# Ten instead of eight groups of a second feed-forward with weight sums made ahead: a decoder layer on one core of Trainium2

## The chip, the cores and the metric

The kernel runs on one core of a Trainium2 chip. The metric is the device time in microseconds (us) of one execution, and the median of several executions is compared. One execution was also taken by the hardware profiler. Its span is the time from the first to the last instruction of the program.

The engines are named as in the profile: PE is the matrix engine (PEld its weight loads), DVE the vector engine, ACT the scalar engine, POOL the general one, and SP the engine whose queue issues nearly all transfers.

## What is computed

The reference is one decoder layer in float32 on 256 tokens of width 2048.

```python
h = layer_norm(alpha * h + 0.5 * swiglu(h, w_ffn1_gu, w_ffn1_down))      # first feed-forward
rq, rk, rv, rg, aq, ak, av, gate_r, gate_a = split(h @ w_in)
ret = (silu(rg) * head_group_norm(retention(rotary(rq), rotary(rk), rv))) @ w_ret_out
att = windowed_attention(rotary(aq), rotary(ak), av, sinks) @ w_att_out
mixed = (sigmoid(gate_r) * ret + sigmoid(gate_a) * att) @ w_mix_out
h = layer_norm(alpha * h + mixed)
h = layer_norm(alpha * h + 0.5 * swiglu(h, w_ffn2_gu, w_ffn2_down))      # second feed-forward
h = layer_norm(alpha * h + sigmoid(h @ w_ple_gate) * (p @ w_ple_proj))
```

There are 8 retention heads, 16 attention heads, and 5632 columns in each feed-forward.

## The kernel before

**Products in float32.** Every float32 operand is split (`split`, L97): ACT casts it to a high part (L98) and DVE subtracts that to get the low part (L99). One product then takes three matmuls (`Sum.add`, L374 to L376). In the profile `hw_in_f` and `lw_in_f` are the high and low parts of a chunk of the input weights; `hf_gu`, `lf_gu` are those of the feed-forward's weights.

**Kinds of weight units.** All weights are listed in `plan` in the order of their use. A pair of blocks of a feed-forward's up projection comes as one of three kinds. A plain pair (P) is two units of `Single`, of 12 matmuls each. `Seven` (S) multiplies the two-by-two blocks with seven products instead of eight, which is 21 matmuls instead of 24. It needs four sums of weight blocks, which DVE forms, ACT casts and DVE splits (L160 to L186). `Prepared` (D) does the same 21 matmuls, but loads the four sums, already split, from DRAM (L198 to L206).

**Sums made ahead.** `sums_ahead` (L219) makes the sums of one or more groups; one group is one D pair of one block. It is a generator that advances by one piece at a time.

```python
        pairs = [[Chunk(k) for k in items[0]]]                 # L226: two loads of 512 KB
        for _ in range(wait):
            yield
        ...
            dve.tensor_tensor(t1, b11, b12, ALU.add)           # L238
            dve.tensor_tensor(t3, b12, b22, ALU.add)           # L239
            act.copy(uh, u)                                    # L240: a cast on ACT
            yield from pause()                                 # `every` times
            dve.tensor_tensor(t2, b11, t3, ALU.add)            # L242
            dve.tensor_tensor(t4, t2, b21, ALU.add)            # L243
            act.copy(vh, v)                                    # L244: a cast on ACT
            ...                                                # L246: loads of the next group
            yield from pause()
            dve.tensor_tensor(ul, u, uh, ALU.subtract)         # L248
```

After another pause DVE makes `vl` (L250) and SP is given two stores of 512 KB (L252). After a last pause come two more (L255), and the next group's L238 follows in the same piece.

**Steps.** The order on every engine is that of the program text. After each weight unit the kernel calls `done`, which issues loads and splits (one cast on ACT and one subtraction on DVE) for units some way ahead, and then `run_side` (L310). `run_side` issues one job of the list `side` and then one piece of the first generator in `lazy`. One such call is called a step here. The generators are queued at L1124 to L1127, and steps are counted from there:

| steps | weight units |
|---|---|
| 1 to 32 | `rqk`: retention's queries and keys |
| 33 to 56 | `rv`: retention's values |
| 57 to 88 | `rg`: retention's gates, eight units for each of four pairs of heads |
| 89 to 92 | `av`: attention's values |
| 93 to 112 | `aqk`: attention's queries and keys, five groups of four |

Before the change the generators take steps 1 to 20 (two groups, `wait` 3, `every` 2), 21 to 31 (a rotary table), 32 to 58 (three groups, 2 and 2) and 59 to 78 (one group, 3 and 4). Two more groups are made during the mixing projection (L1444).

**Side jobs in the gates.** For each pair of heads (h, h+1), nine jobs stand in `side` (L1229 to L1251):

| job | what | steps, by pair of heads |
|---|---|---|
| 1 | scores of h (PE `rs`, DVE `rsc`) | 57, 69, 78, 87 |
| 2 | split of the scores of h (`rsp`), scores of h+1 | 58, 70, 79, 88 |
| 3 | split of the scores of h+1, values of h (PE `ro`, DVE `gst`) | 59, 71, 80, 89 |
| 4 | normalisation of h (DVE, `ron` L1193), values of h+1 | 60, 72, 81, 90 |
| 5 | normalisation of h+1 | 61, 73, 82, 91 |
| 6 | `ron` of h times its gate (DVE L1203) | 65, 74, 83, 92 |
| 7 | transposes of h (PE `rt` L1212), `ron` of h+1 times its gate | 66, 75, 84, 93 |
| 8 | ACT and DVE take h out (`rett`, L1223 and L1224), transposes of h+1 | 67, 76, 85, 94 |
| 9 | the same for h+1 | 68, 77, 86, 95 |

The gate of a pair (`rgs`, L1243) is two ACT instructions, issued after the last of the pair's eight units, and so after the steps 64, 72, 80 and 88.

**Slots.** All these tiles live in 46 slots. `slots_for_weights` tells how many of them the planner (`fill`, L260) may fill with weights. A D pair takes 6 slots to load and 7 while it is used; an S pair takes 2 and 7. In the second feed-forward a block j that has D pairs sets this to 32 minus j (L940), and it stays until the next setting.

**The second feed-forward** has eleven blocks j of its up projection, of 8 pairs each (L839). Even blocks run as PPSSPSSP. Odd ones run as PPSPSPSP, or as PPSDSDSP if they are in `AHEAD_BLOCKS`. Eight transposes (`f2t`, L893) follow two units into the next block.

Of the kernel before, what the change touches and what calls it, by code (L numbers as in the profile page):

```python
# [39 lines left out]


AHEAD = (4, 5)
AHEAD_BLOCKS = (1, 3, 5, 7)
AHEAD_SLOTS = 32

SEVEN_DOWN = (6, 7, 8, 9)
# [9 lines left out]
def layer(ctx: ExitStack, tc: tile.TileContext, io):  # L56
# [16 lines left out]
    def slot(shape, dt, name):  # L73
        return slots.tile(shape, dt, tag="slot", name=name)
# [144 lines left out]
    def sums_ahead(items, wait, every):  # L219


        def pause():
            for _ in range(every):
                yield

        pairs = [[Chunk(k) for k in items[0]]]  # L226
        for _ in range(wait):
            yield
        for j, (key, _) in enumerate(items):
            a, b = pairs.pop()  # L230
            b11, b21, b12, b22 = a.of(a.raw, 0), a.of(a.raw, 1), b.of(b.raw, 0), b.of(b.raw, 1)
            u, v = (slot([P, 2, 512], F32, w + a.name) for w in "uv")
            t1, t3, t2, t4 = (x.rearrange("p (g n) -> p g n", g=2) for x in (u[:, 0], u[:, 1], v[:, 0], v[:, 1]))
            parts = [slot([P, 2, 512], F32R, w + a.name) for w in ("hu", "lu", "hv", "lv")]
            uh, ul, vh, vl = parts
            away = [dram.tile([P, 2, 512], F32, name=f"{w}{a.name}") for w in ("hud", "lud", "hvd", "lvd")]
            put_by_sums[key] = away
            dve.tensor_tensor(t1, b11, b12, ALU.add)  # L238
            dve.tensor_tensor(t3, b12, b22, ALU.add)  # L239
            act.copy(uh, u)  # L240
# [3 lines that stand above are left out]
            act.copy(vh, v)  # L244
            if j + 1 < len(items):
                pairs.append([Chunk(k) for k in items[j + 1]])  # L246
# [3 lines that stand above are left out]
            dve.tensor_tensor(vl, v, vh, ALU.subtract)  # L250
            for e in range(2):
                sync.dma_start(away[e], parts[e].bitcast(F32))  # L252
            yield from pause()
            for e in range(2, 4):
                sync.dma_start(away[e], parts[e].bitcast(F32))  # L255
# [44 lines left out]
    def slots_for_weights(n, ahead=45, far=90):  # L300
        room.update(slots=n, ahead=ahead, far=far)
# [5 lines left out]
    lazy = []  # L307
# [152 lines left out]
    def forms_of(parts, name):  # L460
        hi, lo = (slot([P, 8, P], F32R, name + w) for w in "hl")
        return seven_forms(whole(parts, name + "w"), hi, lo)

    def units_of(order, sevens, ahead=()):

        sevens, ahead = list(sevens), list(ahead)
        plain = [p for p in range(KD // 2) if p not in sevens + ahead]
        of = {"S": sevens, "D": ahead, "P": plain}
        return [(kind, of[kind].pop(0)) for kind in order]
# [369 lines left out]
    def gu_units(name, j):  # L839
        if j == 0:  # L840
            return [("P", p) for p in range(KD // 2)]
        if name == "f2" and j in AHEAD_BLOCKS:
            return units_of("PPSDSDSP", SEVEN[:3], AHEAD)
# [3 lines left out]
    def gu_keys(name, j):  # L847
        return lambda n, p: (name + "_gu", j, n, p)
# [26 lines left out]
    def ffn(name, i, ht, norm, keep, residual, keepers, away):  # L875
# [28 lines left out]
        for j in range(KF // 4):  # L904
# [19 lines left out]
            def before(u, j=j, offset=KD // 2 - len(units)):  # L924
# [7 lines left out]
                if j == 0 and u == 7:  # L932
# [3 lines left out]
                    if name == "f2":  # L936
                        g = AHEAD[0] // 2
                        made[g] = forms_of([ht[:, 4 * g : 4 * g + 4, :]], f"{name}f{g}")
                if name == "f2" and j in AHEAD_BLOCKS and u == 0:
                    slots_for_weights(AHEAD_SLOTS - j)  # L940
# [151 lines left out]
    def mixers(ht, norm, residual, keepers, away):  # L1092
# [29 lines left out]
        slots_for_weights(14)  # L1122
        ahead = [(gu_keys("f2", j)(0, p), gu_keys("f2", j)(1, p)) for j in AHEAD_BLOCKS for p in AHEAD]
        lazy.append(sums_ahead(ahead[:2], 3, 2))  # L1124
        lazy.append(rotary_table("a"))
        lazy.append(sums_ahead(ahead[2:5], 2, 2))
        lazy.append(sums_ahead(ahead[5:6], 3, 4))  # L1127
        for grp in range(8):
            ps = banks(f"rqk{grp}")
            features_out([(("w_in_f", grp), ps)], KD, both_halves)  # L1130
# [310 lines left out]

        lhs = lambda k: of_pairs(mix_t, k)
        slots_for_weights(16)
        lazy.append(sums_ahead(ahead[6:], 3, 2))  # L1444
        for blk in range(3):
            if blk == 2:
                load_for_norm(1)
# [195 lines left out]
    with tc.manual_schedule():  # L1643
        dve.memset(warm, 0.0)
        for eps, v in roots.items():
            dve.memset(v, 4.0 * eps)
        act.activation(warm, warm, AF.Silu)
        plan_ffn("f1")
        plan.extend(Single(("w_pp", blk, 0)) for blk in range(2))
        plan_mixers()  # L1650
        plan.extend(Single(("w_pp", blk, 0)) for blk in range(2, 4))
        plan_ffn("f2")
        for blk in range(4):
            plan_tokens(("w_pg", blk), KD)
        kept = sorted({p // 2 for p in SEVEN})
        warm_up()
        norm = ffn("f1", 0, ht, None, x_parts, x_columns, (), rows[0])
        norm = mixers(norm.new, norm, rows[0], kept, rows[1])
        norm = ffn("f2", 2, norm.new, norm, norm.keep, rows[1], (), None)
        embedding(norm.new, norm, norm.y)  # L1660
        assert not (plan or loaded or ready or side or lazy) and not room["used"]
# [100 lines left out]
```

## Time and profile before

| | before |
|---|---|
| median of 3 runs | 2276.8 us (2276.71 to 2277.43) |
| profiled execution, its own time | 2277.11 us |
| its span | 2275.3 us |
| granted PE clock, mean | 0.999 |

The profile's page gives the busy time of each engine and its share of the span. Matmuls are pipelined, so the duration of one (some 0.39 us) is longer than the distance from one to the next. The view of waits lists for each instruction group which engine it waited for: us in total, times, longest us. The timeline lists instructions in order of time: start us, duration us, engine, line, operation, tile written and tiles read, and in square brackets the engine's idle time before it with what ended it. The chain of waits lists pieces of the path that ended last: start us, us, what.

### The profile page before, as it was taken

What the parts mean: (1) busy time and instruction counts of PE and PEld (TensorE: products, weight loads), DVE (VectorE), ACT (ScalarE), POOL (GpSimd) and SP (SyncE); (2) the same over time, 40 slices, a digit from 0 to 9 for tenths busy, and PEclk for the clock granted to TensorE, in tenths of its full rate; (3) what the DMA queues carried; (4) which work ended last, traced back from release to release, by engine and by line L of the source; (5) the groups of instructions that cost most, each with busy time, mean ns of one, the idle gap of its engine ahead of it and who ended that gap; (6) DMA issues with size and microseconds to landing.
All of it is one profiled execution on the core that took longest, in us unless ns stands there. A gap on an engine that the chain in (4) does not pass through costs nothing.

```text
span 2275.3 us, 29066 instructions
## 1 busy us (share of the span) xinstructions
PE 2263.4 (99%) x10495; PEld 1880.2 (83%) x10495; DVE 1980.6 (87%) x2561; ACT 1219.5 (54%) x1485; POOL 2.2 (0%) x9
## 2 busy tenths in 40 slices
PE   9999999999999999999999999999999999999998
PEld 8888888888888888888778888888888888888876
DVE  7999999999888887787789787789999999889877
ACT  6555555556554444544566454555565556555543
POOL 0000000000000000000000000000000000000000
PEclk9999999999999999999999999999999999999999
DMA  8666665665576789655456568787767766555772
GB/s 300 204 203 198 197 210 179 205 204 189 208 287 247 269 306 306 221 169 165 139 157 224 183 212 273 287 287 237 262 218 250 259 197 216 192 214 190 287 263 75
DMA packets 207592, 505.75 MB, mean 222 GB/s; under 512 B 16076, under 2 KB 19788, under 8 KB 207448
## 3 DMA queue, kind: packets, MB, share of 16 engines
q1 hardware_dynamic: 205320, 501.06, 65.6%
q10 hardware_dynamic: 2128, 2.84, 0.4%
q8 instruction: 82, 1.34, 0.2%
q14 instruction: 62, 0.51, 0.1%
HBM read 478.67 MB, written 25.17 MB: 221 GB/s over the span
## 4 chain that ended last, share of the span: by engine, by line
PE 97%; DVE 1%; DMA 1%; issue 0%; ACT 0%; POOL 0%; ACTq 0%; DVEq 0%; POOLq 0%
PE f1g L375 3%; PE f1g L374 3%; PE f1g L376 3%; PE f2g L376 3%; PE f2g L374 3%; PE f2g L375 3%; PE rqk L325 3%; PE f1u L374 2%; PE f1u L376 2%; PE f1u L375 2%; PE f2u L374 2%; PE f2u L376 2%; PE f2u L375 2%; PE aqk L325 2%; PE f1d L374 2%; PE f1d L376 2%
## 5 line engine op out<-in xcount | busy, mean ns | idle before, releaser
L99 DVE TENSOR_TENSOR lf_gu<-rf_gu,hf_gu 128x1024 fp32r<-128x1024 f32 (+1 forms) x276 | 325.3, 1210 | 13.3 <-ACT hf_gu L98 12.2
L98 ACT CAST hf_gu<-rf_gu 128x1024 fp32r<-128x1024 f32 (+1 forms) x276 | 275.4, 1042 | 30.1 <-DMA rf_gu<-in_f_gu 26.2
L99 DVE TENSOR_TENSOR lf_down<-rf_down,hf_down 128x1024 fp32r<-128x1024 f32 x152 | 181.2, 1219 | 22.6 <-ACT hf_down L98 19.6
L99 DVE TENSOR_TENSOR lw_in_f<-rw_in_f,hw_in_f 128x1024 fp32r<-128x1024 f32 x140 | 167.2, 1218 | 34.5 <-ACT hw_in_f L98 34.5
L98 ACT CAST hf_down<-rf_down 128x1024 fp32r<-128x1024 f32 x152 | 155.4, 1050 | 76.7 <-DMA rf_down<-in_f_down 22.4
L98 ACT CAST huf_gu<-uf_gu 128x1024 fp32r<-128x1024 f32 x70 | 73.7, 1053 | 145.3 <-DVE uf_gu L171 138.8
L98 ACT CAST hw_in_f<-rw_in_f 128x1024 fp32r<-128x1024 f32 x140 | 139.8, 1049 | 2.9 <-DMA rw_in_f<-in_w_in_f 2.3
L374 PE MATMUL f1g<-hf_gu,xt 128*128 128x512 f32 x247 | 96.5, 391 | 0.0
L375 PE MATMUL f1g<-hf_gu,xt 128*128 128x512 f32 x247 | 96.3, 390 | 0.0
L376 PE MATMUL f1g<-lf_gu,xt 128*128 128x512 f32 x247 | 96.3, 390 | 0.0
L98 ACT CAST hvf_gu<-vf_gu 128x1024 fp32r<-128x1024 f32 x70 | 73.8, 1054 | 29.2 <-DVE vf_gu L173 27.8
L950 ACT ACTIVATE eve<-eve 128x1024 f32<-128x1024 f32 x20 | 21.2, 1062 | 126.5 <-DVE eve L949 126.5
L374 PE MATMUL f2g<-hf_gu,ht 128*128 128x512 f32 x223 | 86.9, 390 | 0.0
L376 PE MATMUL f2g<-lf_gu,ht 128*128 128x512 f32 x223 | 86.9, 390 | 0.0
L375 PE MATMUL f2g<-hf_gu,ht 128*128 128x512 f32 x223 | 86.8, 389 | 0.0
L99 DVE TENSOR_TENSOR luf_gu<-uf_gu,huf_gu 128x1024 fp32r<-128x1024 f32 x70 | 85.2, 1218 | 0.0
L99 DVE TENSOR_TENSOR lvf_gu<-vf_gu,hvf_gu 128x1024 fp32r<-128x1024 f32 x70 | 85.2, 1218 | 0.0
L374 PE MATMUL f1u<-hf_gu,xt 128*128 128x512 f32 x212 | 83.5, 394 | 0.0
L376 PE MATMUL f1u<-lf_gu,xt 128*128 128x512 f32 x212 | 82.6, 390 | 0.0
L375 PE MATMUL f1u<-hf_gu,xt 128*128 128x512 f32 x212 | 82.5, 389 | 0.0
L374 PE MATMUL f2u<-hf_gu,ht 128*128 128x512 f32 x180 | 71.3, 396 | 0.0
L376 PE MATMUL f2u<-lf_gu,ht 128*128 128x512 f32 x180 | 70.1, 389 | 0.0
(1439 smaller groups left out, 6511.6 us busy)
## 6 DMA issues: line engine op xcount, KB each, us to landing
rf_gu<-in_f_gu SPq DMA_DIRECT2D x358, 512.0 KB
rf_down<-in_f_down SPq DMA_DIRECT2D x176, 512.0 KB
rw_in_f<-in_w_in_f SPq DMA_DIRECT2D x148, 512.0 KB
rw_rv<-in_w_rv SPq DMA_DIRECT2D x32, 512.0 KB
rw_ret<-in_w_ret SPq DMA_DIRECT2D x32, 512.0 KB
rw_mix<-in_w_mix SPq DMA_DIRECT2D x32, 512.0 KB
rw_pg<-in_w_pg SPq DMA_DIRECT2D x32, 512.0 KB
rw_att<-in_w_att SPq DMA_DIRECT2D x16, 512.0 KB
```

The lines of the kernel that those rows point to most:

```text
L98: act.copy(dst_hi, src)
L99: (lo_engine or dve).tensor_tensor(dst_lo, src, dst_hi, ALU.subtract)
L325: pe.matmul(ps[f], hi[:, kk, f * P : (f + 1) * P], rhs(k), start=k == 0, stop=k == n_k - 1,)
L374: pe.matmul(o, al, bh, start=first, stop=False)
L375: pe.matmul(o, ah, bh, start=False, stop=False)
L376: pe.matmul(o, ah, bl, start=False, stop=self.left == 0)
L950: act.activation(g, g, AF.Silu)
```

## The change

The second feed-forward's block 9 gets two D pairs in place of two plain pairs, so that five blocks with two groups each take prepared sums. The ten groups are made in a new division. The first five stay where they were. The sixth, seventh and eighth are made by one generator that is queued where the sixth was, with `wait` 2 and `every` 3 in place of 3 and 4. The last two are made during the mixing projection, with the same numbers as the last two before.

```diff
 AHEAD = (4, 5)
-AHEAD_BLOCKS = (1, 3, 5, 7)
+AHEAD_BLOCKS = (1, 3, 5, 7, 9)
...
         lazy.append(sums_ahead(ahead[:2], 3, 2))
         lazy.append(rotary_table("a"))
         lazy.append(sums_ahead(ahead[2:5], 2, 2))
-        lazy.append(sums_ahead(ahead[5:6], 3, 4))
+        lazy.append(sums_ahead(ahead[5:8], 2, 3))
...
         slots_for_weights(16)
-        lazy.append(sums_ahead(ahead[6:], 3, 2))
+        lazy.append(sums_ahead(ahead[8:], 3, 2))
```

## The prediction

> **What bounds the kernel now.** I read the page first, then the waits of PE, then the chain.
>
> ```profile
> span 2275.3 us, 29066 instructions
> PE 2263.4 (99%) x10495; PEld 1880.2 (83%) x10495; DVE 1980.6 (87%) x2561; ACT 1219.5 (54%) x1485; POOL 2.2 (0%) x9
> ```
>
> ```profile
> PE plnt L1529 <- DVE plnm L1524: 2.9, 1, 2.9
> ...
> PE rt L1212 <- DVE ron L1203: 0.2, 1, 0.2
> ```
>
> PE is busy for 2263.4 of 2275.3 us, and its longest wait is 2.9 us at the very end. So a matmul taken out is worth its full time, and a new wait of PE costs its full length, since no slack of PE exists later to take it back. Of the few waits one lies where the change adds work: the transposes `rt` of the retention heads wait for DVE's `ron`. DVE is the second engine at 87%.
>
> **What block 9 saves.** In the chain the transposes `f2t` mark the blocks of the second feed-forward. From one mark to the next is one block, from the third unit of one to the second of the next.
>
> ```profile
> 1780.58 0.88 PE f2t L893 x8
> ...
> 1821.59 0.88 PE f2t L893 x8
> ...
> 1863.29 0.88 PE f2t L893 x8
> ...
> 1905.66 0.88 PE f2t L893 x8
> ```
>
> Block 7 with two D pairs takes 1821.59 - 1780.58 = 41.01 us; block 9 without takes 1905.66 - 1863.29 = 42.37. The change makes block 9 like block 7: two pairs of 21 matmuls in place of two of 24, six fewer in all, **-1.36 us**. The left-hand sums that D pairs need exist already.
>
> Does a D pair cost block 9 a wait? Its two pairs load 2.75 MB each (512 + 256 + 4 x 512 KB) in place of 1 MB. In block 7 that shows on DVE, ahead of the S pair that follows the second D pair:
>
> ```profile
> 1795.89 0.69 DVE L170 TENSOR_TENSOR uf_gu<-rf_gu,rf_gu 128x512 f32<-128x512 f32 x1 [4.01 <-DMA rf_gu<-in_f_gu]
> ...
> 1801.50 1.22 DVE L99 TENSOR_TENSOR lvf_gu<-vf_gu,hvf_gu 128x1024 fp32r<-128x1024 f32 x1
> ```
>
> DVE stood idle for 4.01 us and was done with that S pair at 1802.72. At 1.36 / 6 = 0.227 us a matmul, four units of 12 and this one of 21 lie between its beginning and the mark at 1821.59, so PE begins it at 1805.9: 3.2 us in hand, and PE waits for none. Block 9 has 32 - 9 = 23 slots where block 7 has 25, so some of its loads start a unit later. I take 0 for this; the ends are 0 and +1.6 (one unit of 21 matmuls, 4.76 us, less the 3.2 in hand). The two groups during the mixing projection are as many as before: 0.
>
> **What the gates have to take.** The new generator again starts at step 59. With `wait` 2 and `every` 3 a group takes 12 steps: first sums (L238, L239 and a cast) at 61, 73, 85; second sums (L242, L243 and a cast) at 64, 76, 88; `ul` at 67, 79, 91; `vl` at 70, 82, 94. Before, the one group had its pieces at 62, 66, 70 and 74. What two more groups cost DVE is small in sum, and there is room on average:
>
> ```profile
> 918.00:948.00 30.00, 30.00 (x147) 24.96 (x145) 25.08 (x57) 14.43 (x19) 0.00 (x0) 1.00 0.69 219
> 948.00:978.00 30.00, 29.68 (x147) 24.74 (x147) 24.42 (x56) 12.51 (x17) 0.00 (x0) 1.00 0.69 220
> ```
>
> (Columns: stretch, its length, busy PE, PEld, DVE, ACT, POOL, PE clock, DMA share, GB/s.) DVE is busy for about 25 of 30 us; two groups' 10.3 us (each four sums of 0.68 and two subtractions of 1.22) over the 80 us of steps 73 to 97 would fit. But the average hides the order. Each pair of heads has a stretch, from job 3 to job 6, in which DVE has no idle time and PE waits at its end. And each group's casts tie ACT to DVE:
>
> ```profile
> 910.25 0.68 DVE L238 TENSOR_TENSOR uf_gu<-rf_gu,rf_gu 128x512 f32<-128x512 f32 x1
> ...
> 913.66 2.36 DVE L99 TENSOR_TENSOR lw_in_f<-rw_in_f,hw_in_f 128x1024 fp32r<-128x1024 f32 x2 [2.12 <-ACT hw_in_f L98]
> 916.52 1.23 DVE L99 TENSOR_TENSOR lw_in_f<-rw_in_f,hw_in_f 128x1024 fp32r<-128x1024 f32 x1 [0.50 <-ACT hw_in_f L98]
> 917.67 0.68 DVE L1203 TENSOR_TENSOR ron<-ron,rgs 128x512 f32<-128x512 f32 x1
> ...
> 920.00 0.68 DVE L242 TENSOR_TENSOR vf_gu<-rf_gu,uf_gu 128x512 f32<-128x512 f32 x1
> ```
>
> ```profile
> 911.63 1.05 ACT L240 CAST huf_gu<-uf_gu 128x1024 fp32r<-128x1024 f32 x1 [12.01 <-DVE uf_gu L239]
> 912.58 2.00 ACT L98 CAST hw_in_f<-rw_in_f 128x1024 fp32r<-128x1024 f32 x2
> 914.48 1.07 ACT L1243 ACTIVATE rgs<-rg 128x512 f32<-128x512 f32 x2
> 915.45 1.99 ACT L98 CAST hw_in_f<-rw_in_f 128x1024 fp32r<-128x1024 f32 x2
> 921.45 1.05 ACT L244 CAST hvf_gu<-vf_gu 128x1024 fp32r<-128x1024 f32 x1 [4.01 <-DVE vf_gu L243]
> ```
>
> This is the reading that decides. ACT reaches the cast of the sums (L240) 12 us early and stands there; the casts of the next weights are behind it. When DVE has made the sums, ACT casts them, then the weights, and DVE meanwhile idles 2.12 us, because its next instruction in order subtracts those weights. So one pair of sums costs DVE its own 1.4 us and then some 2 us of idling. Before, that fell at step 62, three steps ahead of the next `ron`. The new steps 64, 73 and 88 put it right ahead of one.
>
> PE's arrival at the first transposes of the first, second and fourth pair of heads:
>
> ```profile
> 918.90 0.60 PE L1212 MATMUL rt<-ident,ron 128*128 128x128 f32 x4
> ...
> 948.28 0.66 PE L1212 MATMUL rt<-ident,ron 128*128 128x128 f32 x4 [0.22 <-DVE ron L1203]
> ...
> 1007.29 0.60 PE L1212 MATMUL rt<-ident,ron 128*128 128x128 f32 x4
> ```
>
> PE waits there in order: all units behind stand still with it.
>
> *Heads 0 and 1, step 64.* Last subtraction of step 64 ends its turn at 913.66 + 2 x 1.14 = 915.94. Then, by the distances of the rows above: second sums 1.45 (920.00 to 921.45), cast 0.95 (911.63 to 912.58), the two `rgs` 0.97 (914.48 to 915.45), cast of weights and start of DVE 1.07 (915.45 to 916.52), subtraction 1.15 (916.52 to 917.67), `ron` 0.68. Sum: 922.21, where PE stands ready at 918.90: **+3.3**.
>
> *Heads 2 and 3, step 73.*
>
> ```profile
> 946.40 1.21 DVE L99 TENSOR_TENSOR lw_in_f<-rw_in_f,hw_in_f 128x1024 fp32r<-128x1024 f32 x1
> 947.54 0.68 DVE L1203 TENSOR_TENSOR ron<-ron,rgs 128x512 f32<-128x512 f32 x1
> 948.14 1.22 DVE L250 TENSOR_TENSOR lvf_gu<-vf_gu,hvf_gu 128x1024 fp32r<-128x1024 f32 x1
> ```
>
> The first sums come ahead of the subtraction at 946.40: 1.38 (910.25 to 911.63), cast 0.95, cast of weights 1.08 (912.58 to 913.66), subtraction 1.14, `ron` 0.68: 951.63, against 948.28: **+3.35**. (The `vl` that stood at 948.14, behind `ron`, moves to step 70, where a `ul` of the same length stood.)
>
> *Heads 4 and 5.* `vl` at step 82 lies in the full stretch: +1.14 (a subtraction of that size, 946.40 to 947.54). The second sums at 76 and `ul` at 79 come earlier, where DVE had idle time:
>
> ```profile
> 961.71 0.42 DVE L1153 TENSOR_TENSOR rsc<-rs,dec 128x256 f32<-128x256 f32 x1 [1.15 <-PE rs L1150]
> ...
> 965.53 0.43 DVE L1181 BATCH_NORM_STATS2 gst<-ro 128x6 f32<-128x256 f32 x1 [1.60 <-PE ro L1174]
> ```
>
> Put in there, 1.45 + 2.12 + 1.14 (sums, idling behind them, `ul`) against 1.15 + 1.60 idle and the 1.14 that left step 74 leaves 0.8 at most; I take 0.5. **+1.6**, ends 1.1 and 2.4 (the 1.14 alone; all of the 0.8 and a slip of another 0.5).
>
> *Heads 6 and 7.* Second sums at step 88, again just ahead of `rgs` and of the cast that job 3 needs:
>
> ```profile
> 991.37 0.28 DVE L1154 TENSOR_TENSOR rsc<-rs,dec 128x128 f32<-128x128 f32 x1
> 991.94 1.22 DVE L99 TENSOR_TENSOR lw_in_f<-rw_in_f,hw_in_f 128x1024 fp32r<-128x1024 f32 x1 [0.29 <-ACT hw_in_f L98]
> 993.08 0.55 DVE L99 TENSOR_TENSOR rsp<-rsc,rsp 128x384 fp32r<-128x384 f32 x1
> 994.98 0.43 DVE L1181 BATCH_NORM_STATS2 gst<-ro 128x6 f32<-128x256 f32 x1 [1.34 <-PE ro L1174]
> ...
> 1006.30 0.69 DVE L1203 TENSOR_TENSOR ron<-ron,rgs 128x512 f32<-128x512 f32 x1
> ```
>
> From 991.65: 1.45 + 0.95 + 0.97 + 1.07, subtraction 1.14, split of the scores 0.55: 997.78, where `gst` began at 994.98: 2.8 late. With `ul` at step 91, 1.14, it is 3.9. `ron` was done at 1006.99 and PE came at 1007.29, so 0.3 were in hand: 3.6. The first sums at 85 leave between 0 and 1.4 of theirs; I take 0.4. **+4.0**, ends 2.6 (1.0 less of the chain) and 5.
>
> Sum of the gates: 3.3 + 3.35 + 1.6 + 4.0 = **12.25 us**.
>
> **The queue of SP.** The gates get 4 loads and 8 stores of 512 KB more, block 9 eight loads. SP takes them in order, and a store waits for DVE's low part; what is queued behind is the loads of weights.
>
> ```profile
> SPq L252 <- DVE luf_gu L248: 27.5, 5, 10.4
> ```
>
> SP has waited up to 10.4 us there already, and no weight made PE wait; 6 MB more in 80 us are 75 GB/s beside the 220 of the stretches above. I take 0, with +1 as the end.
>
> **Sum.** 2275.3 - 1.36 + 12.25 = 2286.2 us of span. The profiled execution's own time lay 1.8 above its span, and the median of the runs 0.3 below that time: 2286.2 + 1.8 - 0.3 = **2287.7 us**, 10.9 (0.48%) slower.
>
> **The rivals.**
>
> *DVE's own time only.* If ACT's casts cost DVE no idling, the stages give 1.45 less 0.50 idle and 0.55 in hand = 0.4; 1.2; 1.14; 1.45 + 1.14 less 0.29 + 1.34 + 0.3 idle or in hand = 0.7. That is 3.4 us, or 2278.8. For it: DVE idles 5 of 30 us. Against it: the idle 2.12 behind L239.
>
> *All hidden* (the other side, not slower). The extra 10.3 us of DVE fit into its idle time, and the gain of block 9 stands alone: 2275.4. It decides by whether DVE ever runs late at `rt`; it does now, by 0.22.
>
> *A slower PE after its waits.* The cold start shows it: 19 transposes in 4.31 us, 0.227 each, where eight `f2t` take 0.88, 0.110 each.
>
> ```profile
> 1.44 4.31 PE warm L1641 x19
> ```
>
> If each of the three waits over 3 us brought back such a stretch, half of 4.31 each, 6.5 us: 2294.2. The granted clock of the rows above is 1.00 throughout, and so far PE never waited long enough in mid-kernel to show it. [...]
>
> *Block 9 comes late*, by up to 1.6 instead of saving 1.36: 2289.1 to 2290.7. *The change does nothing in block 9* (plain pairs still used): 2289.1; the plan speaks against it.
>
> **How the numbers follow.** Forecast, from 2285.8 to 2290.5 with the ends of its terms and of SP's queue: 0.62. DVE's own time: 0.13. All hidden: 0.05. Slower PE: 0.09. Block 9 late: 0.09. Nothing done: 0.02. A measurement of this kernel can tell about 0.2%, 4.6 us, from no change: the two hidden cases lie within it, and so does the lowest of the forecast's tail; faster by more would need a gain that no part offers. Faster 0.02, same 0.19, slower 0.79. The range from 2279 to 2293 leaves out the hidden case, most of the slower PE and the tails.
>
> **What would show it.** In the profile of the changed kernel: 10489 matmuls; the marks of block 9 41.0 us apart; `rt` waiting for `ron` about 11 us in four waits, the second and the first near 3.3; ACT standing at L240 or L244 ahead of each. I am wrong if PE's waits in the gates stay under 3 us, if `lf_gu` or `lw_in_f` make PE wait, or if the granted clock falls.

## The result and the profile after

| | before | after |
|---|---|---|
| median of 4 runs each | 2277.11 us (2276.71 to 2277.84) | 2295.65 us (2294.68 to 2297.08) |
| profiled execution, its own time | 2277.11 us | 2294.68 us |
| its span | 2275.3 us | 2292.9 us |
| granted PE clock, mean | 0.999 | 0.996 |

After is slower by 18.5 us: the ratio is 1.0081, with a 95% interval of 1.0069 to 1.0093. The forecast was 10.9 us. The page of after:

```profile
PE 2268.3 (99%) x10489; PEld 1881.8 (82%) x10489; DVE 1988.4 (87%) x2573; ACT 1222.6 (53%) x1489; POOL 2.2 (0%) x9
```

PE runs 10489 matmuls, six fewer, as the plan says. But its busy time rose by 4.9 us (from 2263.4). Fewer matmuls that take longer: that is the first sign that more than waiting was added. The waits of PE come next (us in total, times, longest):

```profile
PE rt L1212 <- DVE ron L1203: 11.1, 4, 3.5
...
PE f210s L374 <- ACT f2a L895: 1.0, 1, 1.0
...
PE ro L1174 <- DVE rsp L99: 0.5, 1, 0.5
```

The four waits at `rt` are there, 11.1 us where before had 0.2, and one of 0.5 at `ro`. `f210s` (a sum of block 10) waits 1.0 for ACT: nothing like it was in before's list.

**How the first wait comes about.** DVE and ACT of after around step 64, by the timeline (start, duration, in brackets the idle time before):

```profile
916.11 0.69 DVE L243 TENSOR_TENSOR vf_gu<-vf_gu,rf_gu 128x512 f32<-128x512 f32 x1
919.88 1.23 DVE L99 TENSOR_TENSOR lw_in_f<-rw_in_f,hw_in_f 128x1024 fp32r<-128x1024 f32 x1 [3.08 <-ACT hw_in_f L98]
921.02 0.68 DVE L1203 TENSOR_TENSOR ron<-ron,rgs 128x512 f32<-128x512 f32 x1
```

```profile
916.89 1.05 ACT L244 CAST hvf_gu<-vf_gu 128x1024 fp32r<-128x1024 f32 x1 [3.04 <-DVE vf_gu L243]
917.84 1.07 ACT L1243 ACTIVATE rgs<-rg 128x512 f32<-128x512 f32 x2
918.81 2.93 ACT L98 CAST hw_in_f<-rw_in_f 128x1024 fp32r<-128x1024 f32 x3
```

Read the two side by side. ACT stands at L244 for 3.04 us, until DVE has made the second sums. Then it casts them, makes both `rgs`, and only then casts the next weights at 918.81. For all of this DVE is idle, 3.08 us, because its next instruction subtracts those weights. `ron` follows at 921.02, and PE has been waiting for it since 918.56 (921.76 less 3.20, in the next rows).

**What the wait leaves behind.** PE of after at that place:

```profile
921.76 0.66 PE L1212 MATMUL rt<-ident,ron 128*128 128x128 f32 x4 [3.20 <-DVE ron L1203]
...
923.23 0.63 PE L375 MATMUL rg<-hw_in_f,ht 128*128 128x512 f32 x1
...
926.22 0.55 PE L376 MATMUL rg<-lw_in_f,ht 128*128 128x512 f32 x1
926.60 0.60 PE L1212 MATMUL rt<-ident,ron 128*128 128x128 f32 x4
```

Do not look at the durations alone, look at the starts. Ahead of the wait the matmuls start 0.227 us apart (sixteen of them from 914.78 to 918.18: 3.40 / 15). From 923.23 to 926.22 lie seven more, all in one row: (926.22 - 923.23) / 7 = 0.43 us. PE is not waiting there; it counts as busy while its matmuls start at about half that rate. Stretches of 5 us show it in the granted clock (columns: stretch, length, PE busy, PE clock, DMA share, GB/s):

```profile
920.00:925.00 5.00, 3.24 (x13) 0.81 0.39 132
925.00:930.00 5.00, 5.00 (x22) 0.85 0.37 107
930.00:935.00 5.00, 5.00 (x24) 1.00 0.92 315
...
955.00:960.00 5.00, 3.98 (x14) 0.73 0.26 66
...
1020.00:1025.00 5.00, 3.20 (x11) 0.71 0.86 256
```

The clock falls after each of the three waits over 3 us and is back at 1.00 at 926.54, 960.67 and 1025.52 (read in stretches of 0.1 us), which is 4.8, 4.7 and 3.7 us after PE resumed. From the transposes at such a wait to the next ones PE takes 4.84 us each time (921.76 to 926.60 in the rows above). Behind the short wait of heads 4 and 5, with as many matmuls in between, it takes 3.25 us (988.05 to 991.30). That is 1.6 us three times, **4.8 us** in all. The mean clock of the whole run, 0.996 against 0.999, hardly shows it.

**Blocks 8 to 10.** The timeline of after has the marks at these starts (they read 0.17 below those of the chain):

```profile
1837.94 1.04 PE L893 MATMUL f2t<-ident,evw 128*128 128x128 f32 x8
...
1879.63 1.04 PE L893 MATMUL f2t<-ident,evw 128*128 128x128 f32 x8
...
1921.06 1.04 PE L893 MATMUL f2t<-ident,evw 128*128 128x128 f32 x8
...
1964.49 1.04 PE L893 MATMUL f2t<-ident,evw 128*128 128x128 f32 x8
```

Block 9 takes 41.43 us (before 42.37, block 7 41.01). Block 10, which the change does not touch, takes 43.43. In before its end has this mark:

```profile
1947.35 0.88 PE f2t L893 x8
```

So it took 1947.35 - 1905.66 = 41.69 us. Both together: 0.8 **more** than before.

The account: the mark of 1821.59 stands at 1837.94 + 0.17 = 1838.11, 16.5 us late. Of that 11.1 - 0.2 + 0.5 = 11.4 are waits in the gates and 4.8 the half rate. Blocks 9 and 10 add 0.8. Sum 17.0 of the 17.6 us between the spans; the other 0.6 was not traced.

### The profile page after: what moved, and what is told of

The parts are those of the page before. It is cut to its first block, busy times and chain, and to the rows that moved or that the text cites. A ratio compares the mean times of both kernels' runs of the same rounds, so it can differ in the third digit from the quotient of the medians.

```text
span 2292.9 us, 29115 instructions
## 1 busy us (share of the span) xinstructions
PE 2268.3 (99%) x10489; PEld 1881.8 (82%) x10489; DVE 1988.4 (87%) x2573; ACT 1222.6 (53%) x1489; POOL 2.2 (0%) x9
## 4 chain that ended last, share of the span: by engine, by line
PE 94%; DVE 4%; DMA 1%; issue 1%; ACT 0%; SPq 0%; POOL 0%; DVEq 0%; ACTq 0%; POOLq 0%
PE f1g L376 3%; PE f1g L374 3%; PE f1g L375 3%; PE rqk L325 3%; PE f1u L374 2%; PE f1u L376 2%; PE f1u L375 2%; PE f2g L376 2%; PE f2g L374 2%; PE f2g L375 2%; PE f2u L374 2%; PE f2u L376 2%; PE f2u L375 2%; PE aqk L325 2%; PE f2d L374 2%; PE f1d L374 2%
## 5 line engine op out<-in xcount | busy, mean ns | idle before, releaser
L374 PE MATMUL f2g<-hf_gu,ht 128*128 128x512 f32 x217 | 84.6, 390 | 0.0
L375 PE MATMUL f2g<-hf_gu,ht 128*128 128x512 f32 x217 | 84.5, 389 | 0.0
```

The source lines that it names most:

```text
L374: pe.matmul(o, al, bh, start=first, stop=False)
L375: pe.matmul(o, ah, bh, start=False, stop=False)
```

## The experiments

The theory after this reading: *(a)* the waits come from ACT's casts of the sums standing in line for DVE; *(b)* waits over about 3 us bring a stretch at half rate; *(c)* block 9's D pairs load too late, and block 10 pays. The rivals: the slowness is that of busy DMA queues or of PE memory banks and not of idling (against b); the gates' work alone is too much for DVE (against a); block 10 suffers from the gates' traffic or by chance (against c).

### gates_only: the groups without block 9

```diff
-        if name == "f2" and j in AHEAD_BLOCKS:
+        if name == "f2" and j in AHEAD_BLOCKS[:4]:
...
-                if name == "f2" and j in AHEAD_BLOCKS and u == 0:
+                if name == "f2" and j in AHEAD_BLOCKS[:4] and u == 0:
```

> All ten groups are made as after the change, but block 9 keeps its plain pairs (the two groups made for it are not used). If the loss lies in the gates (11.4 us of waits at rt and ro, and about 5 us in which the matmuls are 427 ns apart instead of 227), it stays: the marks of the second feed-forward come 16.5 us late, block 9 takes 42.4 us again, and the time is near 2293.6. If block 9's D pairs save their 1.36 us as predicted and the end's loss comes from elsewhere, the time rises by 1.4 over the changed kernel, to 2297.

Measured 2294.23 us (2293.05 to 2297.25), ratio 1.0076 (1.0063 to 1.0090). The waits at `rt` are those of after: 11.1 us in four, the longest 3.5. Nearly the whole loss is made in the gates. The D pairs of block 9 do not save 1.4 on top: by the marks blocks 9 and 10 take 84.08 us here and 84.86 in after. (The medians lie 1.4 us apart, but the four runs of each overlap.) The half rate is not the same each time. After the second wait it held already for the transposes, 1.12 for four where 0.66 is usual:

```profile
954.81 1.12 PE L1212 MATMUL rt<-ident,ron 128*128 128x128 f32 x4 [3.45 <-DVE ron L1203]
```

After the first wait, of 3.21 us, there was none in this run: 3.24 us from those transposes to the next (922.16 to 925.40). After the last, of 3.23 us, it held longest: 5.93 us from those transposes to the next (1020.57 to 1026.50) in place of 3.25. So five of the six waits over 3 us in after and gates_only brought a half-rate stretch.

### block9_only: block 9 without the gates' groups

```diff
-            for w, v in zip(("hu", "lu", "hv", "lv"), put_by_sums.pop(self.key)):
+            for w, v in zip(("hu", "lu", "hv", "lv"), put_by_sums[(self.key[0], min(self.key[1], 7)) + self.key[2:]]):
```

(before, with block 9 added to `AHEAD_BLOCKS`; the generators make the eight groups of before)

> The groups are made as before the change, and block 9's D pairs load the sums that were made for block 7 (so block 9's product is of other weights; the work and the transfers are those of the change). If late loads and a late DVE eat up block 9's saving, marks 8 to 9 and 9 to 10 are 41.4 and 43.4 us apart, PE waits about 1 us in block 10, and the time is 2277.9, 0.8 over before. If block 9 saves what the step said, they are 41.0 and 41.7 and the time is 2275.7.

Measured 2279.02 us, ratio 1.0007 (0.9998 to 1.0016): above both, nearer the theory. The marks and DVE ahead of the S pair that follows the second D pair:

```profile
1864.13 1.04 PE L893 MATMUL f2t<-ident,evw 128*128 128x128 f32 x8
...
1882.67 0.69 DVE L170 TENSOR_TENSOR uf_gu<-rf_gu,rf_gu 128x512 f32<-128x512 f32 x1 [7.01 <-DMA rf_gu<-in_f_gu]
...
1906.23 1.04 PE L893 MATMUL f2t<-ident,evw 128*128 128x128 f32 x8
...
1949.68 1.04 PE L893 MATMUL f2t<-ident,evw 128*128 128x128 f32 x8
```

Block 9 42.10, block 10 43.45: block 10 loses the same 1.7 without anything changed in the gates. DVE stands 7.01 us there for a load; in block 7 it was 4.01. PE in turn waits 0.3 and 0.2 us in block 9's sum `f29s` for `luf_gu` and `lvf_gu`, two of the low parts that DVE makes late.

### filled: PE kept running through the waits

Spare transposes of the identity stand ahead of the `rt` of heads 0, 2 and 6 and write the bank that `rt` then overwrites. They take out no wait of the order, they only keep PE from standing still in it.

```diff
+                for _ in range({0: 26, 2: 28, 6: 26}.get(h, 0)):
+                    pe.transpose(ps[:, 0, :P], ident, ident)
```

> The changed kernel, with 26 to 28 spare transposes of the unit matrix ahead of the first transposes of heads 0, 2 and 6, about 2.9 to 3.1 us of PE work in place of idling. If the half-rate stretches come from PE's idling, they vanish, PE's waits there fall to some 0.3 us each, and the time falls by about 5 us to 2290.5. If they come from something else (the load of DVE and DMA, say), the matmuls behind are still 427 ns apart and the time stays at 2295.6.

Measured 2290.31 us (2288.57 to 2292.99), ratio 1.0058 (1.0044 to 1.0072): 5.3 us below after. PE at step 65, and the clock of the same stretches:

```profile
918.86 3.00 PE L1211 MATMUL rt<-ident 128*128 128x128 f32 x26
922.21 0.66 PE L1214 MATMUL rt<-ident,ron 128*128 128x128 f32 x4 [0.35 <-DVE ron L1203]
```

```profile
920.00:925.00 5.00, 4.65 (x32) 1.00 0.37 140
...
955.00:960.00 5.00, 5.00 (x27) 1.00 0.35 106
...
1020.00:1025.00 5.00, 5.00 (x31) 1.00 0.94 304
```

`ron` comes no earlier (922.21 against 921.76), yet the clock stays at 1.00. More work on PE made the kernel faster. So the half rate comes from PE's standing still, not from the DMA or the work around it, and it is worth some 5 us: (b) holds. One dip is left in this profile, at another place: a wait of 2.04 us of the mixing projection's `lnps` brought it, 0.57 from 1484 to 1488.

### part_filled: how long a wait it takes

The same with 6, 14 and 10 spare transposes, so that shorter waits are left.

> The changed kernel with 6, 14 and 10 spare transposes ahead of the first transposes of heads 0, 2 and 6: PE's waits there shrink from 3.2, 3.45 and 3.2 to about 2.5, 1.9 and 2.1 us, with the end of each wait where it was. If the half rate needs an idle stretch of some 3 us, no matmuls come 427 ns apart and the time is 2290.3, as with all filled. If waits of 2 us bring it too, the time is 2293 to 2295.

Measured 2292.57 us (2289.76 to 2293.58), ratio 1.0064 (1.0048 to 1.0079): between filled and after. The rows of the three waits, with a group of the same eight matmuls ahead of the third and behind it:

```profile
922.67 1.11 PE L1214 MATMUL rt<-ident,ron 128*128 128x128 f32 x4 [2.54 <-DVE ron L1203]
...
956.67 0.66 PE L1214 MATMUL rt<-ident,ron 128*128 128x128 f32 x4 [1.92 <-DVE ron L1203]
...
1014.76 2.00 PE L325 MATMUL aqk<-ht,hw_in_f 128*128 128x512 f32 x8
...
1020.85 0.86 PE L1214 MATMUL rt<-ident,ron 128*128 128x128 f32 x4 [2.04 <-DVE ron L1203]
1021.37 3.56 PE L325 MATMUL aqk<-ht,hw_in_f 128*128 128x512 f32 x8
```

```profile
920.00:925.00 5.00, 2.46 (x10) 0.72 0.35 126
...
955.00:960.00 5.00, 3.33 (x17) 1.00 0.17 55
...
1020.00:1025.00 5.00, 4.15 (x14) 0.66 0.98 309
```

Waits of 2.54 and of 2.04 us brought the half rate, the one of 1.92 did not, nor did the wait of 1.24 in after or those of 1.30 and 1.24 in cast_later, where the clock reads 1.00 from 890 to 1040. The median lies 2.3 us above that of filled, but the four runs of each overlap, so here the rows decide and not the times.

The length of the wait is not all, for the one of 3.21 us in gates_only brought nothing. In stretches of 0.1 us the clock of after reads 0.50 for 3.41 us behind each of its waits of 3.20, 3.45 and 3.22 us, from 923.12, 957.26 and 1022.11 on, which is 1.36, 1.24 and 0.31 us after PE resumed. These starts lie 34.14 and 64.85 us apart, 10 and 19 times 3.41, and in the 3.41 us ahead of each PE had stood still for 2.05, 2.17 and 3.10 us. What decides beside the length, and why the stretch behind the last wait of gates_only was longer (5.93 us in place of 3.25), was not shown.

### cast_later: ACT's cast one step behind DVE's sums

The same sums in the same steps; only the cast on ACT is issued one step later, so that ACT does not stand in front of it.

```diff
             dve.tensor_tensor(t3, b12, b22, ALU.add)
+            yield
             act.copy(uh, u)
-            yield from pause()
+            for _ in range(every - 1):
+                yield
...
-            act.copy(vh, v)
...
-            yield from pause()
+            yield
+            act.copy(vh, v)
+            for _ in range(every - 1):
+                yield
```

> The changed kernel with the two ACT casts of each group one step behind the sums that they read. If ACT standing at those casts, with the casts of weights behind it, makes most of the delay, the waits at rt shrink to DVE's own work (0.4, 1.2, 1.2 and about 1 us), none is long enough for the half rate, and the time is near 2282. If DVE's own extra work makes the delay, the waits stay over 3 us and the time at 2295.

Measured 2280.83 us (2279.67 to 2282.74), ratio 1.0016 (1.0007 to 1.0025): 14.8 us below after, with the same instructions on every engine. ACT at step 64, to be held against the rows of after:

```profile
914.39 1.04 ACT L98 CAST hw_in_f<-rw_in_f 128x1024 fp32r<-128x1024 f32 x1
916.38 1.06 ACT L249 CAST hvf_gu<-vf_gu 128x1024 fp32r<-128x1024 f32 x1 [0.95 <-DVE vf_gu L245]
```

```profile
PE rt L1216 <- DVE ron L1207: 3.4, 3, 1.3
```

The weights' cast at 914.39 now goes ahead of the cast of the sums. Three waits are left, 1.30, 1.24 and 0.82, and no half rate. So (a) holds, and DVE's own added work costs 3.4 us in the gates. Blocks 9 and 10 still lose: 41.61 and 43.42.

### block9_slots25 and block9_slots29: room for block 9's loads

block9_only (with block 7's sums as stand-ins, as there), with more slots in blocks 9 and 10 than the 23 of the formula:

```diff
-                    slots_for_weights(AHEAD_SLOTS - j)
+                    slots_for_weights(AHEAD_SLOTS - j if j < 9 else 25)
```

and the same with 29.

> As the kernel with block 9 alone, but blocks 9 and 10 keep the 25 slots for weights that they had before, in place of 23. Theory: the loads of the second D pair and of the S pair behind it still start when they do in block 7 (about 4 us of DVE idling there), so a part of the loss stays: marks 8 to 10 about 1 us over 41.0 + 41.7, time near 2278. If two slots fewer are the whole cause: 41.0 and 41.7, 2275.9. If the number of slots has no part in it: 2279.

> The same with 29 slots in blocks 9 and 10, as block 3 has. Counted by the planner's rules the second D pair's loads then start 19.7 us ahead of its use in place of 9.5. Theory: DVE idles at most 1 us ahead of the S pair, PE waits nowhere in blocks 9 and 10, marks 41.0 and 41.7 apart, time 2275.9, 1.36 below before. If the 3.5 MB more of transfers are late in themselves, the loss of some 1.5 us stays and the time is near 2279.

25 slots: 2278.93 us, ratio 1.0006 (0.9997 to 1.0015). 29 slots: 2276.12 us, ratio 0.9995 (0.9986 to 1.0004). DVE ahead of the S pair, first with 25, then with 29 slots:

```profile
1881.82 0.69 DVE L170 TENSOR_TENSOR uf_gu<-rf_gu,rf_gu 128x512 f32<-128x512 f32 x1 [6.86 <-DMA rf_gu<-in_f_gu]
```

```profile
1875.87 0.69 DVE L170 TENSOR_TENSOR uf_gu<-rf_gu,rf_gu 128x512 f32<-128x512 f32 x1 [0.80 <-DMA rf_gu<-in_f_gu]
```

The marks with 29 slots:

```profile
1863.44 1.04 PE L893 MATMUL f2t<-ident,evw 128*128 128x128 f32 x8
...
1904.45 1.04 PE L893 MATMUL f2t<-ident,evw 128*128 128x128 f32 x8
...
1946.15 1.04 PE L893 MATMUL f2t<-ident,evw 128*128 128x128 f32 x8
```

With 29 slots block 9 takes 41.01 and block 10 41.70: the full saving of 1.36 us, and block 10's loss is gone. With 25, block 7's own number, nothing is mended: by the marks they take 85.44 us together, as block9_only's 85.55. The loads' start explains both. SP issues the first load of sums of the second D pair 3.4 us behind the mark in block 7 of after (1800.50, mark 1797.09), 5.0 behind it in block 9 (1884.77, mark 1879.80), with 25 slots 5.2 behind it (1868.82, mark 1863.58), and with 29 slots 5.6 **ahead** of it (1857.96, mark 1863.60); the marks here are the chain's.

```profile
1800.50 0.34 SPq L205 DMA_DIRECT2D huf_gu<-hudf_gu  x1
...
1884.77 0.42 SPq L205 DMA_DIRECT2D huf_gu<-hudf_gu  x1
```

So (c) holds. Why 25 slots start the loads later in block 9 than in block 7 was not looked for. Between 2276.12 and before's 2277.38 the measurement can't decide; the marks can.

### placed_slots29: the ten groups, each piece in a step of its choice

All ten groups are made; those of the gates by a copy of the generator that is told the step of each piece. First sums, their cast, second sums, their cast, `ul` and `vl` stand at steps 62, 63, 66, 67, 68, 69; 75, 76, 77, 78, 84, 85; 86, 87, 93, 94, 95, 96: away from the last step ahead of a `ron`. Blocks 9 and 10 have 29 slots.

```diff
-        lazy.append(sums_ahead(ahead[5:8], 2, 3))
+        lazy.append(sums_at(ahead[5:8], 59, ((62, 63, 66, 67, 68, 69), (75, 76, 77, 78, 84, 85), (86, 87, 93, 94, 95, 96))))
```

> All ten groups and block 9's D pairs, mended in two places: the sixth to eighth group's pieces stand at steps 62 to 69, 75 to 85 and 86 to 96, in the jobs 7 to 2 of the heads, with each cast a step behind its sums; blocks 9 and 10 have 29 slots. Theory: the waits at rt fall to 0 to 0.5 us in all, block 9 saves 1.36, and the time is 2275.9, faster than both. If DVE's extra work delays PE wherever it stands, 2279 to 2281.

Measured 2276.88 us (2275.53 to 2277.72), ratio 0.9996 (0.9987 to 1.0005). The stretch that holds the gates:

```profile
890.00:1040.00 150.00, 149.79 (x807) 1.00 0.71 248
```

PE is busy for 149.79 of 150 us and no `rt` waits. With every cost of the change taken out its gain stands alone, and 1.36 us in 2277 is too little to be told from before. No version beats the kernel before by more than can be measured.

## Why the prediction was wrong in its size

The direction and the main mechanism were right; the time came out 8 us above the forecast and beyond the range. Step by step:

- **Waits in the gates: 12.25 forecast, 11.4 measured.** Heads 0 and 1: 3.3 against 3.20. Heads 2 and 3: 3.35 against 3.45. Heads 4 and 5: 1.6 against 1.24. Heads 6 and 7: 4.0 against 3.22 and 0.46 at `ro`. Following DVE and ACT in order through each stretch, with durations from rows, gave each wait to 0.4 us. (That DVE has no idle time from job 3 to job 6 is not so for heads 0 and 1, where the prediction's own rows show 2.12; its sum does not need it there.) cast_later shows the cause, ACT's casts standing in line, and not only the sum; its 3.4 us are also what the rival "DVE's own time only" had for the gates.
- **"PE never waited long enough in mid-kernel to show it": the step that failed.** The rival "a slower PE after its waits" is what came, on top of the forecast: 4.8 us in after, 5.3 by filled, against the 6.5 that the rival had. It stood at 0.09 though the forecast itself held three waits of that size. Waits of 2.04 and 2.54 us were enough in part_filled. That before showed none in mid-kernel was no evidence, for its longest wait there was 0.7 us. And before does show it at its end: behind the 2.9 us wait of `plnt`, which the prediction quotes, its clock falls to half:

```profile
2269.50:2270.00 0.50, 0.50 (x2) 0.62 0.00 0
2270.00:2270.50 0.50, 0.50 (x2) 0.50 0.00 0
```

  The prediction's own signal, a falling granted clock, was the right one.
- **Block 9: -1.36 forecast with ends 0 and +1.6 for lateness; +0.8 measured, 2.16 worse.** The rival "block 9 comes late" (up to +1.6 instead of the saving) had the size, and it too stood at 0.09. The saving itself is real (41.01 with 29 slots). The second D pair's loads do start later, as the prediction said. The step that failed is taking the S pair's 3.2 us in hand as the whole of the matter. In after that S pair is 2.4 us later than in block 7, behind 5.41 us of idling, and by its marks PE loses 0.4 of it in block 9:

```profile
1897.48 0.69 DVE L170 TENSOR_TENSOR uf_gu<-rf_gu,rf_gu 128x512 f32<-128x512 f32 x1 [5.41 <-PE f2g L375]
```

  (The profile ends this idling with PE, where block9_only, with the same D pairs, ends it with the load; with 29 slots 0.80 us of it is left, and 1.05 in placed_slots29.) The rest is lost in block 10. ACT's copies of `f2t` stand behind casts of sums that DVE makes late:

```profile
1925.49 1.05 ACT L98 CAST huf_gu<-uf_gu 128x1024 fp32r<-128x1024 f32 x1 [2.67 <-DVE uf_gu L171]
1926.95 1.05 ACT L98 CAST hvf_gu<-vf_gu 128x1024 fp32r<-128x1024 f32 x1 [0.40 <-PE f2u L376]
1927.90 1.07 ACT L895 COPY f2a<-f2t 128x512 f32<-128x512 f32 x2
```

  They come 6.8 us behind the mark, with 29 slots 4.4 (1908.87 and 1904.45), and PE waits 0.98 for them. That is the order of ACT and DVE which the prediction followed in the gates and did not follow past the end of block 9. The other 0.8 of block 10's 1.74 lies in gaps too small for the list of waits; they went with the lateness, and were not traced one by one.
- **SP's queue: 0 forecast, 0 measured.** No weight of the gates is in the list of PE's waits, and placed_slots29 moves the same 6 MB with PE at 149.79 of 150 us.
- **All hidden** would have needed DVE to be in time at `rt`; the same ten groups in other steps make it so.

Put into the sum for the profiled execution: 2288.0 - 0.85 (waits) + 4.8 (half rate) + 2.16 (block 9) = 2294.1, where it took 2294.68.

## What to carry to other kernels

In the gates a wait of PE of 2.04 to 3.45 us mostly cost its length and 1.3 to 1.6 us more (once 2.7, once nothing), because PE ran at half rate behind it; a forecast that contains such waits should look for that term, whether or not the kernel before showed it in the same place. When two engines in order feed each other, place the instruction that waits (here ACT's cast) behind the work that the other engine needs next: one step of distance was worth 14.8 us, far more than the arithmetic that was added. And when a buffer comes late, follow it to the next stage, not only to its first reader.

## What the runs showed of the hardware

After PE had stood still for 3.20 to 3.45 us (after, gates_only) its matmuls of 512 columns started 0.43 instead of 0.23 us apart until the clock rose again, in after 3.41 us after it fell. That began at once (gates_only, second wait: 1.12 us for four transposes instead of 0.66) or 1.36 us after PE resumed (after, first wait). It came after 2.04 and 2.54 us too (part_filled), was absent once after 3.21 (gates_only) and once after 1.92 (part_filled), and did not come after 1.24 in after or 1.30 in cast_later. The granted clock does not show the slow start: before's first 4 us read 1.00 in it, though the `warm` transposes there take 0.227 us each where `f2t` later take 0.110. Most of the kernels with such waits or their filling also scatter more: after's four runs lie 2.4 us apart, those of part_filled 3.8, of gates_only 4.2 and of filled 4.4, where 27 runs of before lie within 2.1; why is not shown. The profiled run of filled was the slowest of its four; the wait of 2.04 us at `lnps` that the other profiles do not show is part of it, and its cause was not looked for.
